# Rotary embedding on packed rows, and five smaller edits, in a two-block transformer kernel

## The chip, the core and the metric

The kernel runs on one core of a Trainium2 chip. The core has five engines that this document names as the profile does: PE (TensorE, with its weight loads listed apart as PEld), DVE (VectorE), ACT (ScalarE), POOL (GpSimd) and SP (SyncE, which here only issues DMAs). The metric is device microseconds of one execution; lower is better.

## What is computed

The reference applies a block of two attention layers with feed-forward nets, and then one hybrid layer (gated delta rule and linear recurrence). The sequence has 256 positions and 1024 features, all in fp32. What matters here is the start of each of the two attention layers:

```python
def apply_partial_rope(x, cos, sin):          # ROPE_DIM = 16 of 64 features of a head
    half = ROPE_DIM // 2
    x1, x2, rest = x[..., :half], x[..., half:ROPE_DIM], x[..., ROPE_DIM:]
    return jnp.concatenate([x1 * cos - x2 * sin, x2 * cos + x1 * sin, rest], axis=-1)
...
        h = rms_norm(x, norm_mix[l])
        proj = h @ w_in[l]
        dq, dk, dv, sq, sk, sv, gate_logits = jnp.split(proj, splits, axis=-1)
        dq = apply_partial_rope(dq.reshape(dshape), cos, sin)     # 12 heads
        dk = apply_partial_rope(dk.reshape(dshape), cos, sin)     # 12 heads
```

So of the 64 features of each of 24 heads only the first 16 turn, in two halves of 8 that exchange their places.

## The kernel before

Activations are kept with features on partitions: a tile of 128 partitions by 256 positions holds two heads. Every product of an activation with a weight is made of three fp32r matmuls: both factors are split into a high and a low part, and high x high, low x high and high x low are summed. A weight arrives as fp32 by a DMA of 1 MB (`load`, into one of four buffers `raw`, issued by SP) and is split by `convert` into 1024-column tiles `wh` (ACT, six buffers) and `wl` (DVE, five buffers). The split activation is the tile `xx`, made by `new_x`; `xh` and `xl` are its two halves.

A weight chunk has 512 output features (two DMAs). `mm_feat` makes 96 matmuls of 256 columns from it: for each of eight k-blocks, four output tiles times three (`three`). `mm_tok` puts positions on the partitions instead, with 48 matmuls of 512 columns. `mm_pair` makes 64: for each output tile and k-block one of 512 columns (`xx` whole) and one of 256. The feed-forward nets use `mm_pair` up and `three` down.

A layer (`layer1`) multiplies the chunks in the order 3 (queries and keys of the stick-breaking attention, `ps3`), 0, 1, 2 (the 24 heads that turn: `ps0`, `ps1`, `ps2`), 4, 5 (values, `ps4`, `ps5`), and then the gate chunks 6 to 9, whose matmuls lie between those of the attention. Four PSUM buffers `ps` hold two chunks' results.

The rotary embedding of chunk c is in two parts. `rope_in` copies the chunk's result to `q0` on ACT and issues four DMAs from ACT's queue that bring the 8-row halves, exchanged, into the tile `qr`. `rope` multiplies whole 128x512 tiles: `q0` by a cosine on DVE, `qr` by a sine on POOL, and adds them on DVE into `qT` or `kT`; rows that don't turn have cosine 1 and sine 0. The factor `rb` (the norm's 1/rms per position) is in those tables (`cosR`, `sinR`). The tables themselves are made once, by `rope_tables` in the first layer. The scores s_ = qT x kT of the dilated attention wait for all of `qT` and `kT`.

Instructions are recorded in Python's order and then ordered engine by engine by the tile framework's scheduler; each engine and each DMA queue works strictly in its order. The program starts with chunk 3 of layer 0, whose two weight DMAs are cut into eight pieces of 256 KB that alternate with eight 128 KB pieces of the input `x`. Eight small matmuls L304 on zeros run ahead of the first real one.

In the hybrid layer, `level` merges the blocks of a triangular inverse; at its last level (n = 3) the halves of 64 rows are merged.

Of the kernel before, what the change touches and what calls it, by code (L numbers as in the profile page):

```python
# [16 lines left out]
P = 128  # L17
# [39 lines left out]
RP = 2  # L57
# [18 lines left out]
def kernel_body(tc, I, O, tap=lambda *a: None, upto=99):  # L76
# [3 lines left out]
    with ctx:  # L80
# [15 lines left out]
        pos_i = nrm.tile([P, T], I32, name="pos_i", tag="rb", bufs=2)  # L96
        S.dma_start(vec[:, 0:8], I["vec"][:, 0:8])
# [33 lines left out]
        def load(ap, pieces=1, between=()):  # L131
            raw = rawp.tile([P, 2048], F32, name="raw")
            n = 2048 // pieces
            for j in range(pieces):
                D.dma_start(raw[:, n * j:n * j + n], ap[:, n * j:n * j + n])
                if between:
                    between.pop(0)()
            return raw
# [20 lines left out]
        def chunk_w(ap):  # L159

            return cols512(unit(ap[:, 0:2048]) + unit(ap[:, 2048:4096]))

# [143 lines left out]
        first = [lambda j=j: D.dma_start(x[:, j:j + 1], I["xT"][:, j:j + 1]) for j in range(8)]  # L306
        raws = [load(I["w_in"][0, 3, :, 2048 * j:2048 * j + 2048], 4, first) for j in range(2)]
        xh, xl, xx = new_x()
# [11 lines left out]

        def rope_tables():

            ak = nrm.tile([P, 2, T], F32, name="ak", tag="sq", bufs=1)
            a, k = ak[:, 0], ak[:, 1]
            G.tensor_copy(a, pos_i)
# [16 lines left out]
            G.tensor_scalar(cosT, cosT, -1.0, None, op0=OP.add)  # L342
            G.tensor_scalar(cosT, cosT, vc("rope"), 1.0, op0=OP.mult, op1=OP.add)

        cosT = cst1.tile([P, T], F32, name="cosT")
        sinT = cst1.tile([P, T], F32, name="sinT")
# [17 lines left out]
        def layer1(l, xh, xl, xx, nm):  # L364
            with tc.tile_pool(name="gt", bufs=1) as gt:
# [5 lines left out]
                with tc.tile_pool(name="at", bufs=1, reuse_waits="tile") as at, \  # L371
# [7 lines left out]
                    cosR = at.tile([P, T], F32, name="cosR")  # L379
                    sinR = at.tile([P, T], F32, name="sinR")  # L380
                    cb = cosR[:, None, :].to_broadcast([P, 2, T])
                    sb = sinR[:, None, :].to_broadcast([P, 2, T])


                    qr = [at.tile([P, 4, T], F32, name=f"qr{i}") for i in range(2)]
                    for t_ in qr:
                        G.memset(t_, 0.0)
# [12 lines left out]
                    def rope(c, q0):  # L400
                        for j in range(2):
                            mb = 4 * c + 2 * j
                            o = qT[:, mb:mb + 2] if mb < 6 else kT[:, mb - 6:mb - 4]
                            q, r = q0[:, 2 * j:2 * j + 2], qr[c % 2][:, 2 * j:2 * j + 2]
                            V.tensor_tensor(q, q, cb, op=OP.mult)
                            G.tensor_tensor(r, r, sb, op=OP.mult)
                            if mb == 6:
                                V.tensor_tensor(o, q, r, op=OP.add)
                            else:
                                pair = lambda a: a.rearrange("p m (a b) -> p m a b", b=2)  # L410
                                V.tensor_tensor(o.rearrange("p m (b a) -> p m a b", b=2), pair(q), pair(r), op=OP.add)
# [8 lines left out]
                    w0 = unit(I["w_in"][l, 0, :, 0:2048])  # L420
                    if l == 0:
                        D.dma_start(cf, I["cf"])
                    col = rstd_cols(nm, 1e-5, ab, last_lo[0] if AFT else None, parity=True)
                    box = []
                    w0 = cols512(w0 + unit(I["w_in"][l, 0, :, 2048:4096]))
                    if l == 0:
# [3 lines left out]
                        rope_tables()  # L430
                    ps0 = mm_feat(w0, xh, xl, lambda i: i == MIDA and box.append(rows(col, ab)))
# [4 lines left out]
                    V.tensor_tensor(cosR, cosT, rb, op=OP.mult)  # L436
                    V.tensor_tensor(sinR, sinT, rb, op=OP.mult)
# [34 lines left out]
                    rope(0, q0)  # L472
                    stick(0)
                    q1 = rope_in(1, ps1)
                    ps2 = mm_feat(chunk_w(I["w_in"][l, 2]), xh, xl)
                    rope(1, q1)
                    stick(1)
                    q2 = rope_in(2, ps2)
                    ps4 = mm_tok(chunk_w(I["w_in"][l, 4]), xh, xl)
                    ps5 = mm_tok(chunk_w(I["w_in"][l, 5]), xh, xl, parity=True)  # L480
                    vals(0, ps4)
                    rope(2, q2)
# [31 lines left out]
                    for h in (1, 3):  # L514
                        pp_ = [at.tile([P, 4, T], F32, name="p", tag="p", bufs=2) for _ in range(2)]
                        for t in range(2):
# [9 lines left out]
                            for e in range(2):  # L526
# [4 lines left out]
                                V.tensor_scalar(st[:, 1:2], st[:, 0:1], -0.125, None, op0=OP.mult)  # L531
                                act(sm, sm, AF.Exp, bias=st[:, 1:2], scale=0.125, accum_out=st[:, 2:3])
# [59 lines left out]
            with tc.tile_pool(name="ff", bufs=2) as ff, \  # L592
# [57 lines left out]
                xh, xl, xx = new_x()  # L650
# [48 lines left out]
        with tc.tile_pool(name="g1", bufs=1, reuse_waits="tile") as g1, \  # L699
# [218 lines left out]
            def level(n):  # L918
# [4 lines left out]
                for b in range(2):  # L923
                    dg = NP_[:, :, 256 * b:256 * b + 128]
                    py = bank((P, 4, 64))
                    for h in range(4):
                        PE.matmul(kr(py)[:, h], dg[:, h], ev(W[b])[:, h], start=True, stop=True,
                                  skip_group_check=True)
                    Y.append(g1.tile([P, 4, 64], F32, name="Y", tag="Y", bufs=2))
                    V.tensor_tensor(Y[b], py, lvl[n], op=OP.mult)  # L930
                for b in range(2):
# [6 lines left out]
                    else:  # L938
                        pz = bank((64, 4, 64))
                        for h in range(4):  # L940
                            PE.matmul(pz[:, h], Y[b][:, h], Tr[b][:, h, 64:128], start=True, stop=True,
# [258 lines left out]
def layout(a):  # L1200
# [70 lines left out]
    hd = np.arange(P) % 64  # L1271
    put("inv_freq", np.where(hd < 16, np.array(INV_FREQ, f)[hd % 8], 0).astype(f))
    put("sgn", np.where(hd < 8, -1, np.where(hd < 16, 1, 0)).astype(f))
    put("rope", (hd < 16).astype(f))
# [56 lines left out]
```

## Time and profile before

| | |
|---|---|
| time, median of 3 | 1042.65 us (1042.63 to 1044.05) |
| time of the profiled execution | 1043.3 us |
| its span (first to last instruction) | 1041.2 us |
| PE busy | 1028.8 us, 99% |
| DVE, ACT, POOL busy | 825.0, 609.2, 33.3 us |
| TensorE clock granted | 0.999 of full speed |

The span is what the trace shows; 2.1 us of the execution's own time lie outside it. "Busy" for PE means that some matmul was under way. A matmul's length in the trace is not what it costs: matmuls overlap, and the cost of one in a row of matmuls is the distance from its start to the start of the next.

### The profile page before, as it was taken

The page shows a single profiled execution, that of the slowest core. Times are in us where ns is not written, and L with a number is a line of the kernel's source. Part 1 is how long each engine was busy: PE and PEld are TensorE (multiplying, and loading weights), DVE is VectorE, ACT ScalarE, POOL GpSimd, SP SyncE. Part 2 cuts the span into 40 slices and gives each one's busy share as a digit, 9 for nine tenths or more (in the row PEclk, how much of TensorE's full clock was granted, in tenths as well). Part 3 has the DMA queues.
Part 4 walks back from the last instruction along what each step waited for, and adds up shares of the span by engine and source line. Part 5 has one row for each costly group of instructions (what it writes and reads, how often), then busy time and mean ns, then how long its engine had stood idle before and what let it go on. Part 6 is the DMA issues. An engine that isn't in the chain of part 4 may idle for free.

```text
span 1041.2 us, 17297 instructions
## 1 busy us (share of the span) xinstructions
PE 1028.8 (99%) x6950; PEld 934.2 (90%) x6950; DVE 825.0 (79%) x1390; ACT 609.2 (59%) x920; POOL 33.3 (3%) x29
## 2 busy tenths in 40 slices
PE   8999999999999999999999999999999999999997
PEld 7987899899999999878999999999999999888886
DVE  6796678978787878866989877879897998676573
ACT  5556766656556655666666565558648564454452
POOL 1320000000000002100000000000000000000000
PEclk9999999999999999999999999999999999999999
DMA  9553447455464654624455646456433245455541
GB/s 319 177 191 132 163 162 243 128 196 203 164 217 167 222 181 154 206 82 162 161 173 195 219 164 223 172 193 201 164 124 114 82 142 192 173 174 212 181 162 41
DMA packets 28257, 180.31 MB, mean 173 GB/s; under 512 B 3409, under 2 KB 5073, under 8 KB 7185
## 3 DMA queue, kind: packets, MB, share of 16 engines
q1 hardware_dynamic: 27360, 177.90, 49.4%
q10 hardware_dynamic: 816, 1.32, 0.5%
q8 instruction: 54, 0.88, 0.4%
q14 instruction: 27, 0.21, 0.1%
HBM read 177.36 MB, written 1.05 MB: 171 GB/s over the span
## 4 chain that ended last, share of the span: by engine, by line
PE 91%; DVE 5%; DMA 2%; ACT 1%; issue 1%; SPq 0%
PE ps L199 25%; PE ps L200 13%; PE acc L1102 7%; PE ps L166 7%; PE ps L164 7%; PE ps L165 7%; PE acc L165 4%; PE acc L166 4%; PE acc L164 4%; DVE wl L149 2%; PE ps L213 1%; PE ps L214 1%; PE ps L215 1%; DMA raw<-in_w_in 1%; PE acc L1171 1%; PE o L547 1%
## 5 line engine op out<-in xcount | busy, mean ns | idle before, releaser
L149 DVE TENSOR_TENSOR wl<-raw,wh 128x1024 fp32r<-128x1024 f32 x328 | 390.7, 1221 | 41.8 <-PE acc L1102 23.6
L199 PE MATMUL ps<-xx,wh 128*128 128x512 f32 x1184 | 415.9, 394 | 0.0
L148 ACT ACTIVATE wh<-raw 128x1024 fp32r<-128x1024 f32 x328 | 332.7, 1052 | 106.8 <-PE ps L165 54.2
L200 PE MATMUL ps<-xx,wl 128*128 128x256 f32 x1184 | 331.7, 281 | 0.0
L199 PEld LDWEIGHTS ps<-xx,wh 128*128 128x128 f32 x1184 | 221.4, 187 | 48.2 <-DVE t__9760 L1138 0.2
L200 PEld LDWEIGHTS ps<-xx,wl 128*128 128x128 f32 x1184 | 223.7, 189 | 2.0 <-issue 0.3
L164 PE MATMUL ps<-xx,wh 128*128 128x256 f32 x480 | 137.7, 288 | 0.8 <-ACT xx L287 0.8
L165 PE MATMUL ps<-xx,wh 128*128 128x256 f32 x480 | 136.4, 285 | 0.6 <-DVE xx L288 0.5
L166 PE MATMUL ps<-xx,wl 128*128 128x256 f32 x480 | 136.2, 285 | 0.6 <-DVE wl L149 0.5
L165 PE MATMUL acc<-gl,wh 128*128 128x256 f32 x352 | 98.7, 280 | 0.1
L164 PE MATMUL acc<-gh,wh 128*128 128x256 f32 x352 | 98.5, 280 | 0.0
L166 PE MATMUL acc<-gh,wl 128*128 128x256 f32 x352 | 98.5, 280 | 0.0
L164 PEld LDWEIGHTS ps<-xx,wh 128*128 128x128 f32 x480 | 91.8, 191 | 3.0 <-ACT xx L287 1.9
L165 PEld LDWEIGHTS ps<-xx,wh 128*128 128x128 f32 x480 | 91.9, 192 | 1.3 <-DVE xx L288 1.2
L166 PEld LDWEIGHTS ps<-xx,wl 128*128 128x128 f32 x480 | 91.6, 191 | 1.3 <-DVE wl L149 1.2
L616 ACT ACTIVATE lo<-ps 128x256 f32<-128x256 f32 x88 | 33.3, 380 | 59.9 <-PE ps L200 59.8
L164 PEld LDWEIGHTS acc<-gh,wh 128*128 128x128 f32 x352 | 66.1, 188 | 0.8
L165 PEld LDWEIGHTS acc<-gl,wh 128*128 128x128 f32 x352 | 66.2, 188 | 0.5 <-DVE gl L292 0.5
L166 PEld LDWEIGHTS acc<-gh,wl 128*128 128x128 f32 x352 | 66.2, 188 | 0.0
L634 DVE SCALAR_TENSOR_TENSOR cy<-au,vec,cy 128x256 f32<-128x256 f32 x88 | 41.9, 483 | 26.1 <-ACT cy L631 24.8
L617 DVE TENSOR_TENSOR lo<-ps,lo 128x256 f32<-128x256 f32 x88 | 37.0, 422 | 20.4 <-ACT lo L616 19.0
L631 ACT ACTIVATE cy<-au,vec 128x256 f32<-128x256 f32 x44 | 26.0, 600 | 37.4 <-DVE au L618 37.4
(452 smaller groups left out, 1582.0 us busy)
## 6 DMA issues: line engine op xcount, KB each, us to landing
raw<-in_w_in SPq DMA_DIRECT2D x50, 1024.0 KB
raw<-in_w_up SPq DMA_DIRECT2D x44, 1024.0 KB
raw<-in_w_ff SPq DMA_DIRECT2D x32, 1024.0 KB
raw<-in_w_down SPq DMA_DIRECT2D x22, 1024.0 KB
raw<-in_w_out SPq DMA_DIRECT2D x12, 1024.0 KB
raw<-in_w_proj SPq DMA_DIRECT2D x4, 1024.0 KB
raw<-in_w_in SPq DMA_DIRECT2D x8, 256.0 KB
x<-in_xT SPq DMA_DIRECT2D x8, 128.0 KB
```

The source lines that it names most:

```text
L148: S.activation(h, raw[:, j:j + 1024], AF.Copy)
L149: last_lo[0] = V.tensor_tensor(lo, raw[:, j:j + 1024], h.bitcast(F32), op=OP.subtract)
L164: PE.matmul(out, wh, xh, start=start, stop=False, skip_group_check=True)
L165: PE.matmul(out, wh, xl, start=False, stop=False, skip_group_check=True)
L166: PE.matmul(out, wl, xh, start=False, stop=stop, skip_group_check=True)
L199: PE.matmul(o, wh[:, c], xx[:, kb], start=kb == 0, stop=False, skip_group_check=True)
L200: PE.matmul(o[:, 1], wl[:, c], xx[:, kb, 0], start=False, stop=kb == KB - 1, skip_group_check=True)
L616: S.activation(lo, ps[2 * j + i][:, 1], AF.Copy)
L617: V.tensor_tensor(lo, ps[2 * j + i][:, 0], lo, op=OP.add)
L631: S.activation(y[:, j], au[:, j, 2:], AF.Identity, scale=vc("conv_w", f + 2), bias=vc("conv_b", l * 22 + 2 * c + j))
L634: V.scalar_tensor_tensor(y[:, j], au[:, j, k:k + T], vc("conv_w", f + k), y[:, j], op0=OP.mult, op1=OP.add)
L1102: PE.matmul(o, g_[:, kb, ts], w_[:, js], start=False, stop=c == 7 and kb == 3 and n == 2, skip_group_check=True)
```

## The change

The turning rows of eight heads (8 x 16 rows) are brought by eight DMAs into one tile `qp` of 128 partitions, the exchanged halves by two more into `rp`; POOL turns them with three operations of 128x256; eight DMAs put the result back into `qT` or `kT`. All 18 are issued by SP, where before four came from ACT. The rows of `qT` are copied from PSUM by ACT unscaled, those of `kT` by DVE times `rb`; the factor that is now missing in the queries enters the softmax as `qs`, a scale per row. The tables have two variants of 256 positions (for queries and for keys in even-odd order). The weight loads are recorded earlier (`chunk_l`), ahead of the rotary DMAs.

The five smaller edits: the DMAs at the program's start are cut otherwise; `cf` (constants) is loaded ahead of chunk 0; `new_x(40)` lets `xx` begin 40 elements (160 bytes) further on for the inputs of both layers and of the hybrid layer (not for the nets, which call `new_x()`); the queries' scale moves to the softmax, as said; the last `level` uses 64 of 128 rows.

```diff
-        def load(ap, pieces=1, between=()):
-            raw = rawp.tile([P, 2048], F32, name="raw")
...
+        def chunk_l(ap):
+            return [load(ap[:, 0:2048]), load(ap[:, 2048:4096])]
+        def chunk_c(raws):
+            return cols512(convert(raws[0]) + convert(raws[1]))
...
-        def new_x():
-            xx = xp.tile([P, KB, 2, T], F32R, name="xx", tag="xx")
+        def new_x(off=0):
+            xx = xp.tile([P, KB * 2 * T + 40], F32R, name="xx", tag="xx")[:, off:off + KB * 2 * T].rearrange(
+                "p (k w t) -> p k w t", k=KB, w=2)
...
+        S.dma_start(x[:, 0:1], I["xT"][:, 0:1])
         S.dma_start(vec[:, 0:8], I["vec"][:, 0:8])
...
-        raws = [load(I["w_in"][0, 3, :, 2048 * j:2048 * j + 2048], 4, first) for j in range(2)]
-        xh, xl, xx = new_x()
+        for a, b, c, d in ((0, 1, 1, 4), (1, 2, 0, 0), (2, 4, 4, 8), (4, 6, 0, 0), (6, 8, 0, 0)):
+            D.dma_start(raws[a // 4][:, 512 * (a % 4):512 * (a % 4) + 512 * (b - a)],
+                        I["w_in"][0, 3, :, 512 * a:512 * b])
+            if d > c:
+                (S if c == 1 else D).dma_start(x[:, c:d], I["xT"][:, c:d])
+        xh, xl, xx = new_x(40)
...
                     def rope_in(c, ps):
-                        q0 = at.tile([P, 4, T], F32, name="q0", tag="q0", bufs=RP)
-                        for j in range(2):
-                            S.activation(q0[:, 2 * j:2 * j + 2], ps[j], AF.Copy)
-                        for h in (0, 64):
-                            for d in (0, 8):
-                                S.dma_start(qr[c % 2][h + d:h + d + 8], q0[h + 8 - d:h + 16 - d])
-                        return q0
-                    def rope(c, q0):
                         for j in range(2):
                             mb = 4 * c + 2 * j
-                            q, r = q0[:, 2 * j:2 * j + 2], qr[c % 2][:, 2 * j:2 * j + 2]
-                            V.tensor_tensor(q, q, cb, op=OP.mult)
-                            G.tensor_tensor(r, r, sb, op=OP.mult)
-                            if mb == 6:
-                                V.tensor_tensor(o, q, r, op=OP.add)
+                            if mb < 6:
+                                S.activation(halves(qT[:, mb:mb + 2]), eo(ps[j]), AF.Copy)
+                            elif mb == 6:
+                                V.tensor_tensor(kT[:, 0:2], ps[j], rb2, op=OP.mult)
                             else:
-                                V.tensor_tensor(o.rearrange("p m (b a) -> p m a b", b=2), pair(q), pair(r), op=OP.add)
+                                V.tensor_tensor(halves(kT[:, mb - 6:mb - 4]), eo(ps[j]), eo(rb2), op=OP.mult)
+                        q = at.tile([P, T], F32, name="qp", tag="qp", bufs=2)
+                        r = at.tile([P, T], F32, name="rp", tag="rp", bufs=2)
+                        for g in range(8):
+                            D.dma_start(q[g::8], head_rows(c, g))
+                        for h in range(2):
+                            D.dma_start(r[64 * h:64 * h + 64], q[64 - 64 * h:128 - 64 * h])
+                        G.tensor_tensor(q, q, cosT[:, c % 2], op=OP.mult)
+                        G.tensor_tensor(r, r, sinT[:, c % 2], op=OP.mult)
+                        G.tensor_tensor(q, q, r, op=OP.add)
+                        return q
+                    def rope_out(c, q):
+                        for g in range(8):
+                            D.dma_start(head_rows(c, g), q[g::8])
...
+                    raws1 = chunk_l(I["w_in"][l, 1])
                     ps0 = mm_feat(w0, xh, xl, lambda i: i == MIDA and box.append(rows(col, ab)))
...
+                    w1 = chunk_c(raws1)
+                    raws2 = chunk_l(I["w_in"][l, 2])
+                    ps1 = mm_feat(w1, xh, xl)
                     q0 = rope_in(0, ps0)
-                    ps1 = mm_feat(chunk_w(I["w_in"][l, 1]), xh, xl)
...
-                    rope(0, q0)
                     stick(0)
+                    w2 = chunk_c(raws2)
+                    raws4 = chunk_l(I["w_in"][l, 4])
+                    ps2 = mm_feat(w2, xh, xl)
+                    rope_out(0, q0)
                     q1 = rope_in(1, ps1)
...
-                                act(sm, sm, AF.Exp, bias=st[:, 1:2], scale=0.125, accum_out=st[:, 2:3])
+                                act(sm, sm, AF.Exp, bias=st[:, 1:2], scale=qs[:, t:t + 1], accum_out=st[:, 2:3])
...
+                    if n == 6 - LB:
+                        for h in range(4):
+                            PE.matmul(py[64:128, h], dg[0:64, h, 64:128], W[b][0:64, h, 0:64], start=True, stop=True,
+                                      skip_group_check=True)
+                        V.tensor_copy(Y[b][64:128], py[64:128])
+                        continue
```

The built programs show three places. First SP's queue in layer 0, from the loads of chunk 1 (1 MB pieces are 128x2048) on. Before, nothing but weights stands there up to the projection:

```order
L427 DMA vec<-in_vec 128x348
L428 DMA pos_i<-in_pos 128x256
L429 DMA msk<-in_msk 128x1408
L135 DMA raw<-in_w_in 128x2048 x16
L135 DMA raw<-in_w_proj 128x2048 x2
```

With the change the rotary DMAs stand in it (L412 gathers, L414 exchanges halves, L422 puts back; L133 is `load`):

```order
L133 DMA raw<-in_w_in 128x2048 x4
L412 DMA qp<-qT 16x256 x8
L133 DMA raw<-in_w_in 128x2048
L414 DMA rp<-qp 64x256 x2
L133 DMA raw<-in_w_in 128x2048
L422 DMA qT<-qp 16x256 x8
L412 DMA qp<-qT 16x256 x4
L412 DMA qp<-kT 16x256 x4
L133 DMA raw<-in_w_in 128x2048
L414 DMA rp<-qp 64x256 x2
L133 DMA raw<-in_w_in 128x2048
L422 DMA qT<-qp 16x256 x4
```

Chunks 1 and 2 are now loaded ahead of the first gather; each later half chunk stands between two of its steps.

Second, ACT in layer 0 around the evacuation of `ps0` (L392 before, L404 after; L148 and L144 are `convert`, L123 the sines of `rope_tables`). Before:

```order
L148 ACTIVATE wh<-raw 128x1024 x7
L392 ACTIVATE q_465<-ps 128x512 x2
L148 ACTIVATE wh<-raw 128x1024
L395 DMA qr_192<-q_465 8x1024
L123 ACTIVATE sinT<-ak 128x256
L395 DMA qr_192<-q_465 8x1024
L123 ACTIVATE cosT<-ak 128x256
L115 ACT_TABLE_LOAD
L395 DMA qr_192<-q_465 8x1024 x2
L148 ACTIVATE wh<-raw 128x1024 x2
```

With the change:

```order
L144 ACTIVATE wh<-raw 128x1024 x7
L404 ACTIVATE qT<-ps 128x512
L144 ACTIVATE wh<-raw 128x1024
L404 ACTIVATE qT<-ps 128x512
L144 ACTIVATE wh<-raw 128x1024 x2
L123 ACTIVATE sinT<-ak 128x512
L144 ACTIVATE wh<-raw 128x1024
L123 ACTIVATE cosT<-cosT 128x512
L115 ACT_TABLE_LOAD
```

Four conversions now stand ahead of the cosine where one stood before.

Third, PE in layer 0 behind the values: the transposes L493 (L513 after) of the stick-breaking weights, gate matmuls (L199 and L200 before, L201 and L202 after), and `o` (L503, L523), which needs the evacuated transposes. Before, four of the twelve transposes stand 90 rows higher up, and here:

```order
L493 MATMUL pT<-cf,zm 128x128 x8
L199 MATMUL ps<-xx,wh 128x512
L200 MATMUL ps<-xx,wl 128x256
L199 MATMUL ps<-xx,wh 128x512
L200 MATMUL ps<-xx,wl 128x256
L199 MATMUL ps<-xx,wh 128x512
L200 MATMUL ps<-xx,wl 128x256
L199 MATMUL ps<-xx,wh 128x512
L503 MATMUL o<-st_926,vt 64x256 x2
```

With the change:

```order
L513 MATMUL pT<-cf,zm 128x128 x12
L201 MATMUL ps<-xx,wh 128x512
L202 MATMUL ps<-xx,wl 128x256
L201 MATMUL ps<-xx,wh 128x512
L523 MATMUL o<-st_951,vt 64x256 x2
```

Three gate matmuls instead of seven now stand between the last transposes and `o`.

## Rows read from the trace of the kernel before

**Rows 1.** The page: busy time, share of span, instructions; then the granted clock.

```profile
PE 1028.8 (99%) x6950; PEld 934.2 (90%) x6950; DVE 825.0 (79%) x1390; ACT 609.2 (59%) x920; POOL 33.3 (3%) x29
...
PEclk9999999999999999999999999999999999999999
```

**Rows 2.** Waits of PE: who was waited for, us in total, times, longest.

```profile
PE ps L213 <- ACT wh L148: 1.2, 1, 1.2
PE wps L304 <- DVE wz L301: 1.2, 1, 1.2
PE ps L164 <- ACT xx L287: 0.8, 2, 0.6
...
PE ps L166 <- DVE wl L149: 0.5, 1, 0.5
PE ab L264 <- DMA cf<-in_cf: 0.4, 1, 0.4
PE ab L281 <- DVE y L250: 0.2, 1, 0.2
```

**Rows 3.** Timeline of PE in chunk 0 of layer 0: start, length; 105 steps apart.

```profile
28.89 0.28 PE L166 MATMUL ps<-xx,wl 128*128 128x256 f32 x1
...
41.49 0.28 PE L166 MATMUL ps<-xx,wl 128*128 128x256 f32 x1
```

**Rows 4.** Timeline of PE in the down product of layer 0's net; 39 steps apart.

```profile
359.08 0.28 PE L164 MATMUL acc<-gh,wh 128*128 128x256 f32 x1
...
363.66 0.28 PE L164 MATMUL acc<-gh,wh 128*128 128x256 f32 x1
```

**Rows 5.** Timeline of PE in a gate chunk of layer 0; 9 pairs apart.

```profile
124.67 0.39 PE L199 MATMUL ps<-xx,wh 128*128 128x512 f32 x1
...
127.79 0.39 PE L199 MATMUL ps<-xx,wh 128*128 128x512 f32 x1
```

**Rows 6.** The page: two groups of PE's matmuls, with their counts.

```profile
L164 PE MATMUL ps<-xx,wh 128*128 128x256 f32 x480 | 137.7, 288 | 0.8 <-ACT xx L287 0.8
...
L165 PE MATMUL acc<-gl,wh 128*128 128x256 f32 x352 | 98.7, 280 | 0.1
```

**Rows 7.** The chain that ended last, in the last level of the inverse: start, us, what.

```profile
809.50 1.73 PE g L927 x16
...
811.76 1.07 PE g L941 x16
```

**Rows 8.** Timeline of the first 20 us, on ACT, PE and SP.

```profile
6.62 0.63 ACT L291 ACTIVATE wh<-raw 128x512 fp32r<-128x512 f32 x1 [1.67 <-DMA raw<-in_w_in]
8.42 0.39 PE L165 MATMUL ps<-xx,wh 128*128 128x256 f32 x1 [0.34 <-DVE xx L288]
9.08 0.43 SPq L306 DMA_DIRECT2D x<-in_xT  x1
16.40 0.51 ACT L287 ACTIVATE xx<-x,vec 128x256 fp32r<-128x256 f32 x1 [0.98 <-DMA x<-in_xT]
19.50 1.05 PE L264 MATMUL ab<-cf,acc 128*128 128x4 f32 x8 [0.44 <-DMA cf<-in_cf]
```

**Rows 9.** Timeline of DVE in layer 0, the rotary products and sums.

```profile
42.73 3.47 DVE L405 TENSOR_TENSOR q<-q,cosR 128x512 f32<-128x512 f32 x2
46.12 2.04 DVE L411 TENSOR_TENSOR qT<-q,qr 128x512 f32<-128x512 f32 x2
```

**Rows 10.** Layer 1: ACT copies ps0, issues the last qr DMA; POOL starts on it.

```profile
388.00 0.60 ACT L392 ACTIVATE q<-ps 128x512 f32<-128x512 f32 x1 [1.17 <-PE ps L166]
417.79 0.63 ACTq L395 DMA_DIRECT2D qr<-q  x1
423.67 4.56 POOL L406 TENSOR_TENSOR qr<-qr,sinR 128x512 f32<-128x512 f32 x2 [10.77 <-DMA qr<-q]
```

**Rows 11.** All instructions that write qr: duration ns min/median/max.

```profile
L395 ACTq DMA_DIRECT2D qr<-q x24: 631/632/1240, 33.9 to 417.8; - x24
L406 POOL TENSOR_TENSOR qr<-qr,sinR x12: 1301/1744/2313, 42.1 to 425.9; 128x512 f32<-128x512 f32 x12
```

**Rows 12.** The chain that ended last, at the first scores of layer 1.

```profile
440.12 0.41 PE s__4805 L524
```

More of the change, by code (lines that the diff above doesn't have):

```diff
@@ L56 @@
 MIDS = (3, 6)
-RP = 2
 HI = 6
@@ L128, in kernel_body, with load @@
         act_set("silu_and_others")
-        def load(ap, pieces=1, between=()):
+        def load(ap):
             raw = rawp.tile([P, 2048], F32, name="raw")
[L133 to L137, printed above, removed]
+            D.dma_start(raw, ap)
             return raw
@@ L304, in kernel_body @@
             PE.matmul(wps, wz[:, 0:128], wz, start=True, stop=True)
-        first = [lambda j=j: D.dma_start(x[:, j:j + 1], I["xT"][:, j:j + 1]) for j in range(8)]
-        raws = [load(I["w_in"][0, 3, :, 2048 * j:2048 * j + 2048], 4, first) for j in range(2)]
-        xh, xl, xx = new_x()
+        raws = [rawp.tile([P, 2048], F32, name="raw") for _ in range(2)]
+        for a, b, c, d in ((0, 1, 1, 4), (1, 2, 0, 0), (2, 4, 4, 8), (4, 6, 0, 0), (6, 8, 0, 0)):
[4 more added lines that the diff above has]
+        xh, xl, xx = new_x(40)
         nm = Norm()
@@ L319, in kernel_body @@
             nm.add(x[:, 2 * j:2 * j + 2], E=G if PO else V)
+        cosT = cst1.tile([P, 2, T], F32, name="cosT")
+        sinT = cst1.tile([P, 2, T], F32, name="sinT")
         def rope_tables():
-            ak = nrm.tile([P, 2, T], F32, name="ak", tag="sq", bufs=1)
-            a, k = ak[:, 0], ak[:, 1]
-            G.tensor_copy(a, pos_i)
+            a = nrm.tile([P, 2, T], F32, name="ak", tag="sq", bufs=1)
+            k = cosT
+            G.tensor_copy(a[:, 0].rearrange("p (b a) -> p b a", b=2), pos_i.rearrange("p (a b) -> p b a", b=2))
+            G.tensor_copy(k[:, 0], pos_i)
+            G.tensor_tensor(k[:, 0], k[:, 0], a[:, 0], op=OP.subtract)
+            G.tensor_scalar(k[:, 0], k[:, 0], vc("rope"), None, op0=OP.mult)
+            G.tensor_tensor(a[:, 1], k[:, 0], a[:, 0], op=OP.add)
             G.tensor_scalar(a, a, vc("inv_freq"), None, op0=OP.mult)
@@ L435, in layer1 @@
                     V.tensor_tensor(skT, ps3[1], rb2, op=OP.mult)
-                    V.tensor_tensor(cosR, cosT, rb, op=OP.mult)
-                    V.tensor_tensor(sinR, sinT, rb, op=OP.mult)
+                    qs = at.tile([P, 4], F32, name="qs")
+                    V.tensor_scalar(qs[:, 0:2], col[:, 2:4], 0.125, None, op0=OP.mult)
+                    V.tensor_scalar(qs[:, 2:4], col[:, 2:4], -0.125, None, op0=OP.mult)
                     act_set("natural_log_exp_and_others")
+                    w1 = chunk_c(raws1)
+                    raws2 = chunk_l(I["w_in"][l, 2])
+                    ps1 = mm_feat(w1, xh, xl)
                     q0 = rope_in(0, ps0)
-                    ps1 = mm_feat(chunk_w(I["w_in"][l, 1]), xh, xl)
                     zs = []
@@ L530, in layer1 @@
                                                        1.0, -3e38, OP.add, OP.max, st[:, 0:1])
-                                V.tensor_scalar(st[:, 1:2], st[:, 0:1], -0.125, None, op0=OP.mult)
-                                act(sm, sm, AF.Exp, bias=st[:, 1:2], scale=0.125, accum_out=st[:, 2:3])
+                                V.tensor_scalar(st[:, 1:2], st[:, 0:1], qs[:, 2 + t:3 + t], None, op0=OP.mult)
+                                act(sm, sm, AF.Exp, bias=st[:, 1:2], scale=qs[:, t:t + 1], accum_out=st[:, 2:3])
                                 V.reciprocal(st[:, 3:4], st[:, 2:3])
@@ L940, in level @@
                         for h in range(4):
-                            PE.matmul(pz[:, h], Y[b][:, h], Tr[b][:, h, 64:128], start=True, stop=True,
+                            PE.matmul(pz[:, h], Y[b][64:128, h], Tr[b][64:128, h, 64:128], start=True, stop=True,
                                       skip_group_check=True)
@@ L1269, in layout @@
     put("dt_bias", np.broadcast_to(a["gdn_dt_bias_2"][0], (P, 4)))
[L1271 to L1274, printed above, removed]
+    put("inv_freq", np.array(INV_FREQ, f)[np.arange(P) // 8 % 8])
+    put("sgn", np.where(np.arange(P) < 64, -1, 1).astype(f))
+    put("rope", (np.arange(P) % 8 >= 4).astype(f))
     d["vec"] = vec
```

35 lines of the change are left out of this document (14 added, 21 removed).

## The prediction

> **What bounds the kernel now.** First the page [rows 1]. PE is busy 1028.8 of 1041.2 us and the granted clock is full (2.4 GHz) in every slice, so idle time on PE can give back 12.4 us at most, and the rest is matmuls. DVE, ACT and POOL have slack on average; work taken from them is worth only what PE waits for. Next PE's waits [rows 2]: those that touch this change are 1.2 us for ACT's `wh` (L213), 0.5 for DVE's `wl` (L166), 0.4 and 0.2 at the start (`cf`, `y`). None is for `qT`, `kT` or `qr`, so the rotary embedding is hidden today. Last, PE's timeline, for what a matmul costs: 105 steps of chunk 0 take 41.49 − 28.89 = 12.60 us, 120.0 ns each [rows 3]. The same form on `gh` in the down product takes 4.58 us for 39 steps, 117.4 ns [rows 4]. Equal instructions, 2.6 ns apart: that is the largest thing the change can touch.
>
> **The change, part by part.**
>
> *`xx` 160 bytes further on.* In the built program `xx` and the weights `wh` begin, in each partition, at addresses equal modulo 512; `gh` and `wh` differ by 352. With the change `xx` and `wh` differ by 352 too. I take the 2.6 ns for a matter of these places and lower it to 2.4, since one 39-step stretch is a small sample. L164 to L166 are 480 matmuls each on `xx` [rows 6], 1440; of those, 96 belong to the first chunk of `w_ff1`, whose `xx` stays, so 1344 × 2.4 ns = 3.2 us. Bounds: nothing, if the difference lies elsewhere (other products, other loads beside them), and 1344 × 2.6 = 3.5 at the whole difference of the two rows. The gate chunks' pairs (3.12/9 = 347 ns [rows 5], 256 of them) read the moved `xx` too; 2% of 347 either way is ±1.8 us; taken as 0, since no row shows a pair at another place. The nets' hidden tiles (`gh`, `gl`) move as well, by 2208 bytes, to a difference that no row shows: their 3 × 352 matmuls [rows 6] could lose what `xx` gains, 1056 × 2.6 = 2.7 us, or win 0.8; taken as 0.
>
> The Trainium skill (TensorE: Matmul & The Clock Gate, "Step-by-step: what each phase is for") speaks against this term: matmul data and weights come through two independent read ports, and loading the next weights doesn't steal bandwidth from the running matmul. By it the places would not matter, and the term would be 0. The trace doesn't settle it: two forms alike differ, but also in product.
>
> *Last level.* Sixteen L927 take 1.73 us; sixteen L941 of the same stage take 1.07 [rows 7]. On 64 rows the first becomes like the second: −0.66 us, all on the chain that ended last.
>
> *Program start.* Before, ACT waits 1.67 us for its first weight, PE starts at 8.42, `x` block 7 is issued at 9.08 and lands at 16.40, and PE waits 0.44 for `cf` at 19.50 [rows 8]. Now there are fewer and larger pieces, `cf` is ahead of chunk 0, and 0.4 + 0.2 of waits [rows 2] go. Against it: the first matmul needs `x` and `vec`, both now on ACT's queue (one more issue of 0.4 to 0.6 us), and later blocks wait behind larger pieces. Net −0.5, within ±1.5.
>
> *Stalls of layer 0.* The wait at L213 arises because ACT, in order, makes tables and issues `qr` DMAs before a `wh` that PE needs; four conversions now stand ahead of the cosine. The wait at L166 is for `wl` behind DVE's rotary products, 3.47 + 2.04 us a chunk [rows 9], of which only short copies of the keys remain. Both go: −1.65. What is late next is `o`: with three gate matmuls ahead of it rather than seven, two pairs × 0.347 = 0.7 us of cover are gone; taken in full, +0.7 (0 if the evacuation is quicker).
>
> *Tables, softmax scale, POOL.* The tables are twice as wide; `qs` is a small multiply. POOL's busy time of 33.3 us leaves it idle most of the span. Cost 0 while the scores of the dilated attention come later than the tables; they do by far.
>
> *The rotary chain.* Each chunk now takes 8 gathers, 2 exchanges, three POOL operations and 8 put-backs: 18 DMAs, 54 per layer, in SP's order, with two half-chunk loads in between. Its room in layer 1 is from the copy of `ps0` at 388.00 [rows 10] to the first scores at 440.12 [rows 12]: 52.1 us, 51.6 when two chunks (192 matmuls × 2.4 ns) close up. An issue costs between 0.43 (SP [rows 8]) and 0.63 (ACT [rows 10, 11]). The one flight that the trace shows with weights in the air took 423.67 − 417.79 = 5.9 us from issue to POOL's start [rows 10]; I take 2.5 each for gathers and exchange, since many stand behind one another. Two POOL operations after the exchange cost 1.7 (half of 1.744 [rows 11], twice). At 0.47 an issue: 18 × 0.47 + 5 + 1.7 = 15.2 a chunk, 45.5 for three, and some 4 for the copies and the last put-back's flight: 49.5, hidden with 2 us to spare. I take 0.47, SP's own row with a tenth on top, since SP will issue these, and so 0. At 0.63 it is 58.1, 6.5 us too long in each layer.
>
> Sum: −3.2 − 0.7 − 0.5 − 1.65 + 0.7 = −5.3. The profiled execution takes 1043.3 (its span and 2.1 us), which becomes 1038.0; it lay 0.65 above the median of 1042.65, so the median becomes 1037.3.
>
> **Rivals.**
>
> *R1, the places don't matter, or `gh` loses by them.* The matmuls on `xx` stay at 120 ns: −2.1 us in all, 1040.5; with `gh` at 120 as well, 1043.2. For it: the two rows compared are of different products. Against it: they have the same form and the clock is the same.
>
> *R2, on the other side: the scores wait for the rotary chain.* One mechanism: SP issues 54 DMAs in order, and `qT` or `kT` is complete only after the last. For it: the room is only 2 us longer than the chain, and a flight took 5.9 where I reckon 2.5. Against it: SP has nothing else to do, and the loads of chunks 1 and 2 are ahead of the first gather. At 0.55 an issue the chain is 53.8, 2.2 late in each of two layers: 1041.7. Slower than before by 0.2% it is from 0.58 (3.7 late a layer); at 0.60 it is 56.5, 4.9 late: 1047.1; at 0.63, 1050.3. Flights longer by 1.4 us each give the same as 0.60 does. Beside it the Trainium skill (DMA: Bandwidth & Descriptors, "Queues, rings and completion order"): each row of queues has one ring per DMA engine, and an engine goes round-robin between rows. Rotary DMAs moved from ACT's row to SP's thus stand behind weights in the same ring, where before they took turns with them; that can only lengthen the flights, and no row of this trace has a small DMA on SP behind weights outside the start.
>
> **How the numbers follow.** A measurement of this kernel tells some 0.2% (2.1 us) from no change: faster is below 1040.6, slower above 1044.7. The forecast has 0.56, and its own range is 1033 to 1040.5 (the bounds of `xx`, pairs and start together). R1 has 0.17: 0.06 of it just below 1040.6, 0.11 within. R2 has 0.24: 0.05 of a small lateness that ends within 0.2%, 0.19 slower. 0.03 is for things not thought of, counted as the same. So 0.62 faster, 0.19 the same, 0.19 slower. The range is 1032 to 1048: below lies the case of pairs and `xx` both at their best (0.05), above the worse half of R2 (0.1).
>
> **What the profile after would show.** Right: matmuls on `xx` 117 to 118 ns apart in chunk 0 and unchanged in the down product; PE's busy time some 4 us lower; no wait at L213's place nor for `wl`; a wait of some 0.7 us at `o` in layer 0; the last level's first group at 1.07; the scores without a DMA as releaser. Wrong: 120 ns on `xx` (R1), or PE waiting for `qT` or `kT` at the first scores, with SP's last put-back just ahead of them (R2). A gate pair away from 347 ns, or `gh` away from 117.4, would move the sum by the bounds given.

## The result, and the profile after

The changed kernel takes 1071.05 us (median of 4 runs, 1067.63 to 1071.6); beside it the kernel before took 1043.04 (4 runs). The ratio is 1.0265, 95% interval 1.0251 to 1.0278: 28.0 us slower, where 5.3 us faster had been forecast. The profiled execution took 1071.6 us, its span 1069.8.

The page of the changed kernel, the lines that answer to [rows 1]:

```profile
PE 1039.2 (97%) x6950; PEld 938.9 (88%) x6950; DVE 807.0 (75%) x1372; ACT 607.3 (57%) x914; POOL 35.2 (3%) x33
...
PEclk9997999999999999989999999999999999999999
```

PE is busy 10.4 us longer with the same number of matmuls, and idle 30.6 us instead of 12.4. In two slices, early and at the middle, the granted clock is below full. The waits of PE, which answer to [rows 2] (who was waited for, us in total, times, longest):

```profile
PE o L523 <- ACT st L515: 9.3, 2, 5.7
PE ps L201 <- ACT wh L144: 4.6, 1, 4.6
PE pT L557 <- DVE sm L554: 3.3, 1, 3.3
PE ps L166 <- ACT wh L293: 2.7, 1, 2.7
...
PE ps L202 <- DVE wl L145: 1.0, 1, 1.0
```

None is for `qT` or `kT`. New are waits in the attention for weights (`wh`, `wl`) and for `st`, an evacuation that ACT does in order between conversions. The wait for `sm` (3.3 us, at 105.80) has the same root: its exponential on ACT begins at 104.05, behind two conversions that had waited for a weight.

```profile
102.14 2.00 ACT L144 ACTIVATE wh<-raw 128x1024 fp32r<-128x1024 f32 x2 [4.78 <-DMA raw<-in_w_in]
```

The waits of SP's queue show why (the same columns):

```profile
SPq L422 <- POOL qp L417: 38.0, 6, 8.1
```

SP stands 38.0 us at six put-backs (three chunks, two layers) until POOL has turned the rows, and the weight loads that come later in its order stand with it. Its timeline in layer 0 (start, length, what, how many):

```profile
62.12 0.58 SPq L133 DMA_DIRECT2D raw<-in_w_in  x1
70.12 2.42 SPq L422 DMA_DIRECT2D qT<-qp  x4
72.59 2.48 SPq L422 DMA_DIRECT2D kT<-qp  x4
75.17 5.27 SPq L412 DMA_DIRECT2D qp<-kT  x8
80.55 0.52 SPq L133 DMA_DIRECT2D raw<-in_w_in  x1
81.78 1.14 SPq L414 DMA_DIRECT2D rp<-qp  x2
82.97 0.58 SPq L133 DMA_DIRECT2D raw<-in_w_in  x1
91.66 4.95 SPq L422 DMA_DIRECT2D kT<-qp  x8
96.71 2.26 SPq L133 DMA_DIRECT2D raw<-in_w_in  x4
```

Eight put-backs take 4.95 us, 0.62 each. No weight is issued from 62.7 to 80.55, nor from 83.6 to 96.71. Of the first gap SP stands 7.4 us (62.70 to 70.12) and spends the rest on rotary DMAs; of the second it stands 8.1. The chain that ended last names the links of the second gap (start, us, what):

```profile
82.33 4.91 DMA rp<-qp
...
88.30 1.68 POOL rp L416
...
90.04 1.60 POOL qp L417
...
91.66 0.53 SPq L422
...
96.71 5.34 DMA raw<-in_w_in
```

PE, in the same place, waits first for the weight whose load was issued at 80.55, then for `st`:

```profile
87.91 0.49 PE L201 MATMUL ps<-xx,wh 128*128 128x512 f32 x1 [4.63 <-ACT wh L144]
89.43 0.58 PE L202 MATMUL ps<-xx,wl 128*128 128x256 f32 x1 [1.03 <-DVE wl L145]
...
94.10 1.12 PE L523 MATMUL o<-st,vt 128*64 128x256 f32 x4 [3.66 <-ACT st L515]
```

What follows the idle time is dearer too. Windows of that stretch (length, busy time and number of PE, PEld, DVE, ACT, POOL, granted clock, DMA share, GB/s):

```profile
82.00:88.00 6.00, 1.37 (x13) 1.13 (x11) 0.11 (x1) 1.20 (x2) 0.43 (x1) 1.00 0.91 333
88.00:94.00 6.00, 1.42 (x3) 0.60 (x3) 5.85 (x4) 4.89 (x8) 3.56 (x3) 0.53 0.07 26
94.00:99.00 5.00, 4.90 (x29) 3.50 (x30) 0.96 (x3) 1.30 (x4) 0.00 (x0) 0.54 0.31 61
```

PE is idle for most of 82 to 94 us; the granted clock falls to 0.53 (near the lower level, 1.2 GHz), and PE works on at about that until past 98.

The steps that the forecast had named: in chunk 0 of layer 0 the products on `xx` are 117.3 ns apart (105 steps in 12.32 us; [rows 3] had 120.0), and the last level's group is down to 1.07 us ([rows 7]):

```profile
29.26 0.28 PE L168 MATMUL ps<-xx,wl 128*128 128x256 f32 x1
...
41.58 0.28 PE L168 MATMUL ps<-xx,wl 128*128 128x256 f32 x1
```

```profile
836.34 1.07 PE g L950 x16
```

So two of the gains came, and more than 28 us were lost elsewhere.

### The profile page after: what moved, and what is told of

The parts are those of the page before. It is cut to its first block, busy times and chain, and to the rows that moved or that the text cites. A ratio compares the mean times of both kernels' runs of the same rounds, so it can differ in the third digit from the quotient of the medians.

```text
span 1069.8 us, 17378 instructions
## 1 busy us (share of the span) xinstructions
PE 1039.2 (97%) x6950; PEld 938.9 (88%) x6950; DVE 807.0 (75%) x1372; ACT 607.3 (57%) x914; POOL 35.2 (3%) x33
## 4 chain that ended last, share of the span: by engine, by line
PE 86%; DVE 4%; DMA 3%; SPq 3%; ACT 2%; issue 1%; POOL 1%; ACTq 0%; POOLq 0%
PE ps L201 24%; PE ps L202 13%; PE acc L1129 7%; PE ps L166 7%; PE ps L167 7%; PE ps L168 6%; PE acc L167 4%; PE acc L166 4%; PE acc L168 4%; DMA raw<-in_w_in 2%; SPq L422 1%; DVE wl L145 1%; SPq L412 1%; PE acc L1198 1%; PE o L567 1%
## 5 line engine op out<-in xcount | busy, mean ns | idle before, releaser
L145 DVE TENSOR_TENSOR wl<-raw,wh 128x1024 fp32r<-128x1024 f32 x328 | 394.9, 1230 | 72.1 <-ACT wh L144 27.7
L201 PE MATMUL ps<-xx,wh 128*128 128x512 f32 x1184 | 418.8, 397 | 4.6 <-ACT wh L144 4.6
L144 ACT ACTIVATE wh<-raw 128x1024 fp32r<-128x1024 f32 x328 | 333.3, 1052 | 138.7 <-PE ps L167 63.8
L202 PE MATMUL ps<-xx,wl 128*128 128x256 f32 x1184 | 334.0, 283 | 1.0 <-DVE wl L145 1.0
L201 PEld LDWEIGHTS ps<-xx,wh 128*128 128x128 f32 x1184 | 222.8, 188 | 55.0 <-ACT wh L144 4.9
L202 PEld LDWEIGHTS ps<-xx,wl 128*128 128x128 f32 x1184 | 224.4, 190 | 3.7 <-DVE wl L145 1.3
```

The lines of the kernel that those rows point to most:

```text
L144: S.activation(h, raw[:, j:j + 1024], AF.Copy)
L145: last_lo[0] = V.tensor_tensor(lo, raw[:, j:j + 1024], h.bitcast(F32), op=OP.subtract)
L201: PE.matmul(o, wh[:, c], xx[:, kb], start=kb == 0, stop=False, skip_group_check=True)
L202: PE.matmul(o[:, 1], wl[:, c], xx[:, kb, 0], start=False, stop=kb == KB - 1, skip_group_check=True)
```

## The experiments

Two theories stood after the result. L: weights are late, because their loads stand in SP's order behind rotary DMAs that wait. S (the prediction's R2): the scores wait for the rotary chain. Times are medians; "before" is the kernel before on the same chip.

**The rotary DMAs on POOL's queue.**

```diff
-                            D.dma_start(q[g::8], head_rows(c, g))
+                            G.dma_start(q[g::8], head_rows(c, g))
...
-                            D.dma_start(r[64 * h:64 * h + 64], q[64 - 64 * h:128 - 64 * h])
+                            G.dma_start(r[64 * h:64 * h + 64], q[64 - 64 * h:128 - 64 * h])
...
-                            D.dma_start(head_rows(c, g), q[g::8])
+                            G.dma_start(head_rows(c, g), q[g::8])
```

> The changed kernel with its 18 rotary DMAs per chunk on POOL's queue instead of SP's; all else is the same, so SP issues weights alone again. Theory L (the weight loads are late because they stand in SP's order behind rotary DMAs that wait): the wait of PE for wh of 4.6 us and for wl of 1.0 in layer 0 and the longer layer 1 go, 15 to 25 us come back, 1046 to 1056. Rival S (the scores wait for the chain, which is long on any queue): no more than 5 us come back, above 1066, and PE waits for qT or kT at the first scores. Between them, if POOL's own issues make the chain longer than SP's: the loads are on time and the scores late.

1059.51 us (before 1042.79; ratio 1.0163, 1.0147 to 1.0178): 11.5 us came back, less than L had said and more than S. Its waits of PE:

```profile
PE s__987 L544 <- DMA kT<-qp: 7.7, 2, 7.0
...
PE s__4861 L544 <- DMA kT<-qp: 0.9, 1, 0.9
```

The waits for `wh` and `st` in the attention are gone, as L says, and in their place the scores wait, as S says: this is the case that the expectation had put between the two. With one queue for all, the chain is too long. L is not all of it, but S shows only once L is out of the way.

**Put-backs that nobody waits for.**

```diff
-                            D.dma_start(head_rows(c, g), q[g::8])
+                            D.dma_start(sk[64 * (g % 2):64 * (g % 2) + 16, 4 * c + g // 2], q[g::8])
```

> The changed kernel, but the last 8 DMAs of each chunk write a tile that nobody reads, so the scores wait for no rotary DMA, while SP's order and its waits stay (the scores are then of rows that have not turned). Theory L: no change, 1066 to 1073, with the same waits of PE for wh and wl. Rival S: 1043 to 1050.

1069.46 us (ratio 1.0257, 1.0241 to 1.0274), with 7.9 us of waits for `st`, 4.1 for `wh`, 1.2 for `wl`. Taking the scores' wait away changed next to nothing. Between the two this decides for L in the kernel as it was changed.

**Half the small DMAs.**

```diff
-                        for g in range(8):
+                        for g in range(0, 8, 2):
                             D.dma_start(q[g::8], head_rows(c, g))
...
-                        for g in range(8):
+                        for g in range(0, 8, 2):
                             D.dma_start(head_rows(c, g), q[g::8])
```

(`qp` is then two fixed tiles, set to zero once a layer.)

> The changed kernel with 4 gathers and 4 put-backs per chunk on SP instead of 8 and 8, so that half the heads don't turn. Theory L, with a point from which it decides (the chain takes 20.5 us a chunk, 15.5 with half, and PE needs a chunk's weights every 12 to 17 us): the weights are on time, 1046 to 1051. Rival (what counts is that small DMAs stand in SP's queue at all, or the clock): the loss falls by half at most, 1058 to 1065.

1054.41 us (before 1042.35; ratio 1.0115, 1.0101 to 1.0128), between the two ranges, so neither came out. Layer 1 had no long wait any more; layer 0 still had one wait of 7.1 us at `o`. SP and then ACT there:

```profile
70.80 0.53 SPq L133 DMA_DIRECT2D raw<-in_w_in  x1
78.41 2.42 SPq L426 DMA_DIRECT2D kT<-qp  x4
80.95 2.51 SPq L133 DMA_DIRECT2D raw<-in_w_in  x4
```

```profile
86.19 1.06 ACT L144 ACTIVATE wh<-raw 128x1024 fp32r<-128x1024 f32 x1 [6.42 <-DMA raw<-in_w_in]
...
89.24 1.08 ACT L519 ACTIVATE st<-pT 128x512 f32<-128x512 f32 x2
```

The gate chunk's weight stands behind the last put-back (80.95), ACT waits for it, and the evacuation `st` that PE needs is queued behind on ACT, though its own input, the transposes that PE began at 80.55, is ready. So it is not the number of small DMAs alone, but what waits at the head of an in-order queue.

**Half on POOL, half on ACT.**

```diff
-                            D.dma_start(q[g::8], head_rows(c, g))
+                            (S if g % 2 else G).dma_start(q[g::8], head_rows(c, g))
...
-                            D.dma_start(head_rows(c, g), q[g::8])
+                            (S if g % 2 else G).dma_start(head_rows(c, g), q[g::8])
```

(The exchanges are shared likewise.)

> The changed kernel with its rotary DMAs shared between POOL's and ACT's queues, half each, so SP issues weights alone and the chain has half the issues one after the other (some 5 us less per chunk than on POOL alone). Theory L+S (the loss is what SP's late weights cost, and when they are on time, what a chain of over 50 us costs at the scores): the 8 us of waits at the scores of layer 0 go and nearly all comes back that four smaller edits don't cost, 1046 to 1050. Rival (ACT, in order, holds conversions back behind DMAs that wait for POOL): PE waits for wh, 1053 or more.

1064.37 us (ratio 1.0213, 1.0199 to 1.0227): the rival's time came out, though PE waits for `st` and `wl` and not for `wh`. On ACT a conversion now stands behind put-backs, which begin when POOL's last operation has ended (80.43):

```profile
80.46 2.44 ACTq L422 DMA_DIRECT2D kT<-qp  x4
82.95 1.06 ACT L144 ACTIVATE wh<-raw 128x1024 fp32r<-128x1024 f32 x1 [5.63 <-issue]
```

PE waits 7.8 us for `st` and 3.9 for `wl`. A put-back at the head of ACT's order holds back there what it held back at the head of SP's.

**Put-backs alone on POOL's queue**, behind the operation whose result they carry; gathers and exchanges stay on SP.

```diff
-                            D.dma_start(head_rows(c, g), q[g::8])
+                            G.dma_start(head_rows(c, g), q[g::8])
```

> The changed kernel with the 8 put-backs per chunk on POOL's queue, behind the POOL operation whose result they carry; gathers and exchanges stay on SP. Theory L2 (the loss comes from what SP waits for at the put-backs, with the weight loads behind it, and from the serial length of the chain; now SP waits for POOL no more, and gathers of a chunk overlap the put-backs of the one before, so that weights and scores are both on time): 1046 to 1050, no wait of over 2 us in either layer. Rival (ten small DMAs per chunk ahead of weights on SP are enough to make them late): 1053 to 1062, with waits for wh or st.

1044.90 us (before 1042.25; ratio 1.0023, 1.0014 to 1.0032), a little under the range of L2. One engine's name on one line takes back 25 us (28.0 above the kernel before became 2.65). The last issues on SP and on POOL in layer 0, and PE at the scores:

```profile
64.54 1.14 SPq L414 DMA_DIRECT2D rp<-qp  x2
65.72 14.97 SPq L133 DMA_DIRECT2D raw<-in_w_in  x5
```

```profile
78.49 1.92 POOL L422 DMA_DIRECT2D kT<-qp  x4 [0.15 <-DVE wl L145]
```

```profile
85.88 0.48 PE L544 MATMUL s__987<-kT,qT 64*128 64x256 f32 x1
```

Gathers of a chunk no longer wait for the put-backs of the one before; the last put-back is issued at 80.4, 5 us ahead of the scores, and the weights are on time. PE's list has only the start's waits, two of 0.3 us, and one of 0.4 in the hybrid layer: those for `wh` (L213) and `wl` of [rows 2] are gone, and there is none at `o`. The exchange flew as long as in the changed kernel (4.7 us at the median in both), so the loss didn't lie in that flight. The line takes two things off SP: the standing (38.0 us), and the issuing of 48 put-backs (48 × 0.62 = 30 us). How the 25 us divide between them is not shown; gathers and exchanges stayed ahead of weights on SP without a wait of PE for them.

**160 bytes ahead of `xx`, alone on the kernel before.**

```diff
+            xx = xp.tile([P, KB * 2 * T + 40], F32R, name="xx", tag="xx")[:, off:off + KB * 2 * T].rearrange(
+                "p (k w t) -> p k w t", k=KB, w=2)
...
+        xh, xl, xx = new_x(40)
```

> The kernel before with the 160 bytes ahead of xx alone; the tiles behind xx move by 160 bytes too. Theory P (places set the cadence of the products on xx): matmuls of 256 columns on xx at 117.5 to 119 ns instead of 120, -2 to -3 us; pairs of the nets and the products behind them may lose up to 3 us where their tiles moved. Rival (places do nothing): all cadences and the time within 0.5 us of before.

1045.61 us (before 1042.79; ratio 1.0028, 1.0018 to 1.0038): 2.8 us slower, more than P allowed. That the other tiles' loss outweighs `xx`'s gain is shown by the next two runs.

**`xx` alone, and the other tiles alone.** In the first the tile is 512 bytes longer, and what lies behind it keeps its place modulo 512; in the second it is 160 bytes longer and `xx` stays. (The diffs are against the run before this.)

```diff
-            xx = xp.tile([P, KB * 2 * T + 40], F32R, name="xx", tag="xx")[:, off:off + KB * 2 * T].rearrange(
+            xx = xp.tile([P, KB * 2 * T + 128], F32R, name="xx", tag="xx")[:, off:off + KB * 2 * T].rearrange(
```

> The kernel before with the 160 bytes ahead of xx, but the tile made 512 bytes longer instead of 160, so that every tile behind it keeps its place modulo 512. Theory P (the 160 bytes help the products on xx by 3 us, and hurt the nets and the hybrid layer's products by some 5 because the other tiles move against each other): matmuls of 256 columns on xx 117.5 to 119 ns apart as with 160 bytes, pairs and down products as before, 1039 to 1040.5. Rival (the loss of 2.8 us came with xx's own move, or with something that no place explains): 1042.5 or more.

```diff
-        xh, xl, xx = new_x(40)
+        xh, xl, xx = new_x()
```

> The kernel before with the tile of xx 160 bytes longer, but xx at its old place in it: only the tiles behind it move. Theory P: the loss alone, 1046 to 1049, with pairs of the nets at 350 ns instead of 345, the hybrid layer's down products at 231 to 236 instead of 228, and the products of 256 columns on xx as before. Rival: 1042 to 1043.5.

`xx` alone: 1041.04 us (before 1041.89; ratio 0.9992, 0.9983 to 1.0001), a gain no larger than what can be told, less than P had said. The other tiles alone: 1046.26 (ratio 1.0039, 1.0026 to 1.0052), 4.4 us lost, as P had said. The same product in both, 105 steps apart, with `xx` moved (layer 1), then with `xx` in its old place (layer 0):

```profile
380.17 0.28 PE L166 MATMUL ps<-xx,wl 128*128 128x256 f32 x1
...
392.49 0.28 PE L166 MATMUL ps<-xx,wl 128*128 128x256 f32 x1
```

```profile
27.43 0.28 PE L166 MATMUL ps<-xx,wl 128*128 128x256 f32 x1
...
40.03 0.28 PE L166 MATMUL ps<-xx,wl 128*128 128x256 f32 x1
```

12.32 us are 117.3 ns a step, 12.60 are 120.0. Over all stretches of 20 us in the two layers the first run has 117.3 to 118.4 and the second 119.8 to 120.0: the cadence follows the place of `xx`, and not that of the tiles behind it.

**Only the norm's small tiles moved.**

```diff
+        padp = ctx.enter_context(tc.tile_pool(name="padp", bufs=1))
+        padp.tile([P, 88], F32, name="gap")
```

> As the kernel in which only the tiles behind xx move by 160 bytes, but a gap of 352 bytes behind the small tiles of the norm (acc, rb, sq) gives all later tiles their old places modulo 512, so that only those small tiles move. Theory N (the nets lose by their own tiles, gh, lo, au, bu): 1042 to 1043, nothing lost. Rival (they lose by acc, to which they add all along): 1045 or more.

1042.73 us (before 1042.35; ratio 1.0003, 0.9994 to 1.0012): nothing lost. So the 4.4 us come with the tiles behind those, of the layers, the nets and the hybrid layer. Pairs of layer 1's net, 20 steps apart, first with those tiles at their old places, then (the run before) moved by 160 bytes:

```profile
611.71 0.39 PE L201 MATMUL ps<-xx,wh 128*128 128x512 f32 x1
...
618.64 0.39 PE L201 MATMUL ps<-xx,wh 128*128 128x512 f32 x1
```

```profile
612.61 0.39 PE L199 MATMUL ps<-xx,wh 128*128 128x512 f32 x1
...
619.67 0.40 PE L199 MATMUL ps<-xx,wh 128*128 128x512 f32 x1
```

6.93/20 = 346.5 ns against 7.06/20 = 353.0, though `xx`, `wh` and `wl` of these pairs lie where they lay.

The traces of all runs say more of these pairs. In mean over a net (some 330 pairs) they take either 347 to 348 ns or 352 to 353, and 5 ns a pair are 1.7 us a net. With the layers' and nets' tiles at their old places modulo 512, all twelve nets of six kernels are at the lower value. With them moved by 160 bytes, fifteen of eighteen nets are at the higher. But in the run with put-backs on POOL both nets are at the lower (347.6 and 347.5), and every tile lies there where it lies in the changed kernel (352.4). In the run of the start alone, where no tile moves, the gate pairs of layer 1 are at 353.0 (347.9 in the kernel before). So the places matter, but they alone don't set which value a stretch takes; what else does is open. Steadier is the hybrid layer's down product (384 matmuls of 512 columns): 87.2 us in the kernel before, 89.3 with the other tiles moved, 89.4 in the run with put-backs on POOL.

**The program's start alone on the kernel before** (with `cf` ahead of chunk 0).

```diff
+        S.dma_start(x[:, 0:1], I["xT"][:, 0:1])
         S.dma_start(vec[:, 0:8], I["vec"][:, 0:8])
...
+        for a, b, c, d in ((0, 1, 1, 4), (1, 2, 0, 0), (2, 4, 4, 8), (4, 6, 0, 0), (6, 8, 0, 0)):
```

> The kernel before with the edit of the program's start and cf ahead of chunk 0 alone. Theory A (PE waits 3 us for the first wh, as in the run of four edits, and half of it comes back where PE waited for ACT in layer 0): 1043 to 1044.5. Rival (the prediction's: fewer pieces and no wait for cf or y): 1041 to 1042.5.

1043.87 us (before 1041.89; ratio 1.002, 1.0011 to 1.0028): 2 us slower, as theory A had it. ACT's first work, then PE's first product and the pace of those behind it; last the first product of the kernel before:

```profile
6.68 0.51 ACT L288 ACTIVATE xx<-x,vec 128x256 fp32r<-128x256 f32 x1 [3.73 <-DMA vec<-in_vec]
7.10 1.13 ACT L292 ACTIVATE wh<-raw 128x512 fp32r<-128x512 f32 x2
```

```profile
7.76 0.58 PE L165 MATMUL ps<-xx,wh 128*128 128x256 f32 x1 [2.98 <-ACT wh L292]
8.14 0.41 PE L166 MATMUL ps<-xx,wh 128*128 128x256 f32 x1
...
12.41 0.38 PE L165 MATMUL ps<-xx,wh 128*128 128x256 f32 x1
```

```profile
5.00 0.50 PE L164 MATMUL ps<-xx,wh 128*128 128x256 f32 x2 [0.21 <-ACT xx L287]
```

ACT can't begin before `vec`, now issued second, has landed, and the first `wh` stands behind `xx` on ACT. The delay is not all: 20 steps take 12.41 − 8.14 = 4.27 us, 0.21 each, where [rows 3] have 0.12, so 1.9 us more go. The granted clock reads full in that stretch, so the rows don't say why.

**Four edits, old rotary** (start, `cf`, 160 bytes, last level, as in the diff of the change).

> The kernel before with four of the smaller edits (start, cf, 160 bytes ahead of xx, last level), with the old rotary embedding. If the loss is all the rotary's (theory L and rival S alike): 1038 to 1044. If the smaller edits hold a part of the loss (start 1 us later, nets slower): 1044 to 1048.

1046.59 us (before 1042.79; ratio 1.0031, 1.0013 to 1.0049): 3.8 us of the 28 are theirs, as the second forecast had it.

**Three edits, places kept** (`xx` in the tile 512 bytes longer, `cf` ahead of chunk 0, last level).

> The kernel before with three edits: xx 160 bytes further on in a tile that is 512 bytes longer, cf ahead of chunk 0, last level on 64 rows. Theory P: 0.5 to 1.2 us below the run with xx alone, 1038 to 1040, faster than before by 0.3%. Rival: within 0.2% of before.

1041.08 us (before 1041.89; ratio 0.9995, 0.9986 to 1.0003). The rival came out: the last level's gain, 0.66 us in its own group, can't be told in the time.

**All of the change, mended**: put-backs on POOL, the tile 512 bytes longer, the start as before.

```diff
-            xx = xp.tile([P, KB * 2 * T + 40], F32R, name="xx", tag="xx")[:, off:off + KB * 2 * T].rearrange(
+            xx = xp.tile([P, KB * 2 * T + 128], F32R, name="xx", tag="xx")[:, off:off + KB * 2 * T].rearrange(
...
-                            D.dma_start(head_rows(c, g), q[g::8])
+                            G.dma_start(head_rows(c, g), q[g::8])
...
+            D.dma_start(x[:, a:a + 1], I["xT"][:, a:a + 1])
```

> The run with put-backs on POOL, with the tile of xx 512 bytes longer instead of 160 and the program's start cut as before the change. Theory L2 with the placement and start costs as measured (4 and 2 us) taken off: 1040 to 1043. If the rotary's relief of DVE is worth the 1.65 us that the prediction gave it: below 1040.5. Rival as for the other run: 1047 or more.

1040.88 us (before 1042.25; ratio 0.999, 0.998 to 1.0): 1.4 us below the kernel before, with an interval that just reaches no change. It is the fastest version against its own "before" here; whether it beats it stays at the edge of what can be told. The time lies in L2's range and not below 1040.5, and three edits with the old rotary embedding had already given 0.8: a gain from the new rotary embedding itself is not shown.

## Why the prediction was wrong

The account of the 28.0 us, each run against its own "before": with put-backs on POOL 2.65 are left, so put-backs on SP go with 25.4; with places and start mended −1.4 are left, so these two go with 4.0 (alone they had cost 4.4 and 2.0); −1.4 is the change without them. Not all of the 25.4 need be late weights: some 3 us of it are the nets' pairs, 670 at 352.4 ns in one profiled execution and at 347.6 in the other, with every tile in the same place.

*The rotary chain* is the step that failed. I took 0 for it, on two counts. I compared it with the scores alone, while the step itself said that half-chunk loads stand "in between" in SP's order; I never asked what is late when those wait. R2 has the right queue and the wrong victim: its price of up to 1050.3 counts scores that start late, while SP's 38.0 us of standing at put-backs starved the conversions, and through ACT's order the evacuation `st`. (Its flights "longer by 1.4 us each" should read 1.2: six flights for 7.0 us.) And I put an issue at 0.47 us, from SP's loads of `x`; a DMA of 16 rows took 0.62 on SP, the end that I had set aside. The flight of the exchange took 4.7 us at the median against 2.5 (the gathers' 1.8). Behind it stand three POOL operations and not two, since the first writes over `qp`, which the exchange reads; they took up to 1.8 us each against 0.87, and 4.1 in all in the second gap (87.57 to 91.64) against 1.7. A chunk took some 20 to 21 us of SP's time instead of 15.2.

By the Trainium skill (DMA: Bandwidth & Descriptors, "Queues, rings and completion order") a row of queues has one ring on each DMA engine, and the prediction concluded that flights on SP's row would get longer behind weights. The runs don't bear that out: the exchange's 4.7 us are less than the 5.9 of the one flight from ACT's queue before [rows 10], and they are the same in the run that lost nothing by them. The loss was on the issuing side.

*`xx` 160 bytes further on*: right for the cadence. 117.3 to 118.4 ns were measured where 117.4 was the model, and the two runs with `xx` and the other tiles moved apart rule out R1's first half for the cadence: places do matter. Its 3.2 us were 0.85 in time, though (interval from a loss of 0.1 to a gain of 1.8). For *the tiles behind it* I took 0 and bounded the loss by the 256-column products on `gh` (+2.7). It was 4.4, and hardly any of it there (the products on `gh` and `gl` took 0.3 us longer in all): some 2 us lie in the hybrid layer's down product and most of the rest in the pairs, two terms that the prediction did not name. Why a pair slows when none of its own tiles moved is not settled. The Trainium skill (TensorE: Matmul & The Clock Gate, "Step-by-step: what each phase is for") says that weight loads don't steal read bandwidth from the running matmul, by which, the prediction said, places would not matter. They do, with 120.0 and 117.3 ns for one product; whether weight loads have a part in that no run shows.

*Program start*: −0.5 ± 1.5 forecast, +2.0 measured; the delay of the first product that I had named against it (0.4 to 0.6 us) is 2.8: in the trace of before that product starts at 5.00 us, in the run of the start alone at 7.76. The prediction had misread the rows: 8.42 is a later product, and the wait of 1.67 is that of ACT's second weight. The slower pace behind it was not in the sum at all.

*Stalls of layer 0*: right about what goes (both waits are gone in the run with put-backs on POOL), and the 0.7 us at `o` did not come there; the 1.65 us can't be told in the time. *Last level*: right in its group, not visible in the time.

## What to carry to other kernels

When small DMAs are moved to a queue, ask first what waits at its head and what is behind it: a DMA that waits for an engine's result belongs on the queue of that engine, not on the one that feeds the weights. Price the whole chain from rows of its own kind of DMA, and when none exists take the dear end. When a tile grows, keep the places of the tiles behind it, or measure them apart: here the loss of 4.4 us that came with the neighbours' move outweighed the gain that the move was for.

## What was not expected of the hardware

- A pair in the nets takes 347 to 348 ns or 352 to 353 in mean over a net. Where tiles that it doesn't read lay 160 bytes further on, it was the higher value in fifteen of eighteen nets, and the lower in three.
- After PE had been idle for most of 6 us (busy 1.37 us from 82 to 88), the granted clock was 0.53 and 0.54 over the next 11 us. The matmuls from the first `o` to the next gate matmul took 4.69 us there (94.10 to 98.79), and 2.58 in the run with put-backs on POOL (84.38 to 86.96, granted clock 1.00), so 2.1 us of the loss came after the waits were over.
- One put-back of 16 rows of 1 KB takes SP 0.62 us to issue, and POOL 0.48 (1.92 us for four).
